# Local attention in one transformer layer pair: one more head pair as a batch of four query blocks, and a shift of one transpose step

## The chip, the cores and the metric

The kernel runs on one core of a Trainium2 chip. The metric is device microseconds per execution, measured over several runs. A core has TensorE (PE in the profile), VectorE (DVE), ScalarE (ACT), GpSimd (POOL) and SyncE (SP, which here issues most DMAs). PE works on matrices of up to 128 rows and writes to PSUM, which has eight banks of 128 x 512 float32.

## The reference

Two layers, each of: a SwiGLU feed-forward, layer norm, a token mixer, layer norm, a second feed-forward, layer norm. The sequence is 512 tokens of width 1024. The token mixer has three branches of 8 heads of width 64: NSA (compressed, selected and windowed attention), SWA (local attention in windows of 128 with a sink), and FOX (attention with a forget gate). Two of them matter here. Local attention, cut to its core:

```python
kk, vv = with_prev(k), with_prev(v)              # block before, and own block
logits = einsum('bnqghd,bnkgd->bghnqk', q, kk) * scale
logits = where(mask, logits + bias, -inf)
p = softmax(concatenate([logits, sink], -1))[..., :-1]
o = einsum('bghnqk,bnkgd->bnqghd', p, vv)
```

and the compression of NSA's keys and values, whose result the NSA branch needs before its first scores:

```python
flat = blocks.reshape(B, G, nc, CMP_BLOCK * dh)  # 32 positions x 64
return gelu(flat @ w1) @ w2                      # 2048 x 256, 256 x 64
```

## The kernel before

The kernel is one long list of instructions written with a tile framework. `tc.manual_schedule(engines={PE, POOL})` (L89) keeps PE's and POOL's instructions in the order in which the program lists them; a planner orders those of ACT, DVE and SP, with earlier listed instructions ranked higher. Tiles come from tags: a tag has a fixed number of slots, which are used again and again. The tag `p` has 13 slots (`PB`, L753) and serves the probability tiles of all branches, the compression weights (`cw1`, `cw2`), their inputs (`z`) and the GELU's tiles (`gl`, `glt`).

In `mix`, the attention of all branches and the projections that feed it run together. Projections are cut into chunks of 128 columns, each of eight parts of three products (`pj`, 0.7 us a part), and stand in one queue, `fill`. `pump(n)` runs n parts from its head. Some entries of the queue are free: they run with the part behind them and aren't counted.

Attention runs in batches of units. A unit of local attention is `Swa(m, qb)`: head pair m (0 to 3), query block qb (0 to 3). Its `s` makes scores (`sS`, into PSUM tag `sc` with three banks) and the softmax on DVE, ACT and POOL; its `tr` transposes the probabilities on PE (`ptS`, into PSUM tag `tp` with two banks) and evacuates them; its `pv` multiplies by the values (`po`). `step(cur, prev, n)` (L1417) interleaves the scores of batch `cur`, the transposes of the batch before, `prev`, and n pumped parts. It divides them into slots: one score product per slot, then about half of the slot's pumped parts, then transposes in pairs, then the other half. At the end `values()` (L1440) multiplies the batch before by its values. If `prev` is local attention and there are more than twice as many slots as pairs of transposes, the step is `early`: transposes go in the middle slots, and `values()` after the second last slot. `PUMPS` (L1472) says how many parts each step pumps. The batches before are: head pairs 0 and 1 as two batches of two query blocks each, head pairs 2 and 3 as one batch of four each, then thirteen steps of Fox and NSA units.

The compression is fed between. `conv` (L915) takes `cw1` in 16 pieces k, each of two DMAs (L930) and a product into PSUM tile `hid` (L937). `feed` (L962) issues one piece's loads if fewer than four pieces wait in `narrow`. Free entries that call it stand in the queue before each part of the second and third chunk of local queries behind the first two (CQB2, CQB3) and of the first Fox query and key chunks (L1366 to L1369), and nowhere else. `values()` runs what waits in `narrow`, after the value products (L1445). The entry that closes the compression, `end` (L968), is put into the queue five parts before the end of the first NSA query chunk (L1373). It feeds and multiplies what is left, and then transposes the result of the GELU (`glT`, L951). The GELU's five instructions (L941 to L945) are listed behind the product of the last piece, k = 15.

The selected-key chunks of NSA (CKV2, CKV4) come before that query chunk. Each is evacuated into two `hl` tiles (L829 on ACT, L830 on DVE) and copied into its key tile by eight DMAs on SP (L836).

Of the kernel before, what the change touches and what calls it, by code (L numbers as in the profile page):

```python
# [66 lines left out]
def body(tc, a, out, depth=DEPTH):  # L67
# [15 lines left out]
    def ps(tag=None, name="ps", shape=(P, 512)):  # L83
        if tag is None:
            tag = PS_ALL[ring[0] % 8]
            ring[0] += 1
        return psp.tile(list(shape), F32, name=name, tag=tag, bufs=PS_TAGS[tag])
# [663 lines left out]
    def mix(l, wts, pend, done_ffn, xap, xa, nxt):  # L751
# [585 lines left out]
        def pump(n=1):  # L1337
            while n > 0 and fill:
                n -= fill.popleft()() is not FREE
# [58 lines left out]
        def need(u):  # L1398
            if u.br == 1:
                return u.m in m.qb and hasattr(m, "kb")  # L1400
            if u.br == 2:
                return u.m in m.qc and u.m in m.kc and u.m in m.vc and u.m in m.nck
            return u.m in m.qa and hasattr(m, "c2")

        batches = []
        for i in range(4):
            u = [Swa(i, qb) for qb in range(4)]
            batches += [u[0:2], u[2:4]] if i < 2 else [u]
        for i in range(4):
            batches.append([c(i, qb) for qb in (0, 1) for c in (Fox, Nsa)])  # L1410
            batches += [[Fox(i, qb), Nsa(i, qb)] for qb in (2, 3)]
# [1 line left out]
        def chain(gens):  # L1413
            for g in gens:
                yield from g

        def step(cur, prev, n):  # L1417


            for u in cur:  # L1420
                while not need(u):
                    pump(1)
                    n -= 1
            it, iu = chain(u.tr() for u in prev), chain(u.s() for u in cur)
            nt, ns = sum(u.ngrp for u in prev), sum(u.nseg for u in cur)
            pair = 2
            nt = (nt + pair - 1) // pair
            both = 2 if ns == 2 else 1
            ns //= both
            slots = max(nt, ns, 1)  # L1430
            done = 0

            def upto(x):
                nonlocal done
                x = int(round(x))
                if x > done:
                    pump(x - done)
                    done = x

            def values():  # L1440
                if prev:
                    po = ps("po", "po", (P, 4, P))
                    for j, u in enumerate(prev):
                        u.pv(po[:, j])
                    while narrow:  # L1445
                        narrow.popleft()()
                    for j, u in enumerate(prev):
                        nc.scalar.activation(o_t[u.br][u.m][:, u.qb * P:(u.qb + 1) * P], po[:, j], AF.Copy)

            early = prev and isinstance(prev[0], Swa) and slots > 2 * nt  # L1450
            last = min(2, max(n, 0))
            n -= last
            for j in range(slots):
                if j * ns // slots != (j + 1) * ns // slots or slots == ns:
                    for _ in range(both):
                        next(iu, None)
                upto(n * (2 * j + 1) / (2 * slots))
                if (abs(j - slots // 2) < 2 if early else j * nt // slots != (j + 1) * nt // slots or slots == nt):
                    for _ in range(pair):
                        next(it, None)  # L1460
                upto(n * (j + 1) / slots)
                if early and j == slots - 2:
                    values()
            for _ in iu:
                pass
            for _ in it:
                pass
            pump(last)
            if not early:
                values()  # L1470

        PUMPS = [13, 13, 9, 9, 18, 18] + [11, 10, 11] * 4 + [8]  # L1472
        for cur, prev, n in zip(batches + [[]], [[]] + batches, PUMPS):
            step(cur, prev, n)
        while fill:
# [34 lines left out]
        early = deque(["sc", "tp", "sc", "tp", "sc"])  # L1510
# [251 lines left out]
    for l in range(depth):  # L1762
        fin = l == depth - 1
        wts, pend, done, xap, xa = ffn(l, a["ffn1_w1"][l], a["ffn1_w2"][l], 0, xap, xa, wts, pend, done, False,
                                       lambda: mix_first(l), None if l else late)
        wts, pend, done, xap, xa = mix(l, wts, pend, done, xap, xa, lambda: ffn_first(a["ffn2_w1"][l]))
        wts, pend, done, xap, xa = ffn(l, a["ffn2_w1"][l], a["ffn2_w2"][l], 2, xap, xa, wts, pend, done, fin,
                                       lambda: None if fin else ffn_first(a["ffn1_w1"][l + 1]))
# [30 lines left out]
```

## Time and profile before

| | |
|---|---|
| median of three runs | 2409.51 us (2409.47 to 2410.24) |
| the profiled execution | 2409.0 us |
| its span, first to last instruction | 2407.3 us |
| PE busy | 2397.4 us, 100% of the span |
| PE weight loads busy | 2161.8 us, 90% |
| DVE busy | 1960.1 us, 81% |
| ACT busy | 1237.6 us, 51% |
| POOL busy | 298.7 us, 12% |
| granted clock of PE, mean | 0.999 |
| DMA | 319.84 MB, mean 133 GB/s |

Products on PE are pipelined and their ends are modelled, so that a busy PE isn't PE at its peak; the start of one row to the start of the next says more than a row's duration. In a timeline row the columns are start, duration, engine, source line, operation, output and inputs, shape, number of merged instructions, and in brackets the idle time before it and what ended it. A row of the waits is: who waited, on whom, total us, times, longest. SPq is SP's queue of DMA issues; its rows give the issue, not the transfer. PE rows of 32-bit products count each product twice, as it is run in two passes. Layer 0's mixer begins its local attention at about 394 us, layer 1's some 1195 us later.

### The profile page before, as it was taken

Reading aid. Unit: us, or ns where it says so; the run is one execution under the profiler, and the core shown is the slowest. Engines: PE = TensorE matmul, PEld = TensorE weight load, DVE = VectorE, ACT = ScalarE, POOL = GpSimd, SP = SyncE. Lnnn points to the kernel's source line nnn. Section 1 sums busy time; section 2 is a strip of 40 time slices with the busy share of each in tenths; the row PEclk is TensorE's granted clock in tenths of the full one; section 3 lists DMA queues with packets and bytes.
Section 4 is the critical chain, followed back from the end, with each engine's and each line's share of the span. In section 5 each row is a group of like instructions: output and inputs, shape, how many; then the busy total and the mean of one; then the engine's idle time right before and its main releaser. Section 6 shows DMA issues by size and latency. Waiting matters only on the chain.

```text
span 2407.3 us, 42309 instructions
## 1 busy us (share of the span) xinstructions
PE 2397.4 (100%) x16129; PEld 2161.8 (90%) x16129; DVE 1960.1 (81%) x3834; ACT 1237.6 (51%) x2257; POOL 298.7 (12%) x514
## 2 busy tenths in 40 slices
PE   9999999999999999999999999999999999999998
PEld 9999888888889899998899998878888898999987
DVE  7997975787688689888799979667777886898796
ACT  4444644576644435445444446445766444444463
POOL 2000322133300000001100002121332000000021
PEclk9999999999999999999999999999999999999999
DMA  6332975632134433337733339645321344233394
GB/s 204 103 109 90 256 212 162 176 93 81 45 105 132 136 102 114 106 115 211 200 106 108 112 111 243 195 132 150 101 74 55 104 133 147 89 115 106 97 238 147
DMA packets 402155, 319.84 MB, mean 133 GB/s; under 512 B 18536, under 2 KB 348664, under 8 KB 401952
## 3 DMA queue, kind: packets, MB, share of 16 engines
q1 hardware_dynamic: 381424, 267.07, 37.3%
q0 software_dynamic: 20528, 50.07, 9.0%
q8 instruction: 127, 2.08, 0.4%
q14 instruction: 76, 0.62, 0.1%
HBM read 289.77 MB, written 17.88 MB: 128 GB/s over the span
## 4 chain that ended last, share of the span: by engine, by line
PE 99%; DMA 0%; DVE 0%; issue 0%; POOL 0%; SPq 0%; POOLq 0%; ACT 0%; DVEq 0%
PE pg L382 22%; PE acc L487 13%; PE pu L382 11%; PE acc L195 9%; PE pj L181 6%; PE pj L183 6%; PE pj L182 6%; PE pv L382 6%; PE brp L181 2%; PE brp L182 2%; PE brp L183 2%; PE sN L1187 2%; PE ptN L1229 1%; PE po L1248 1%; PE po L1135 1%; PE sF L1104 1%
## 5 line engine op out<-in xcount | busy, mean ns | idle before, releaser
L161 DVE TENSOR_TENSOR lo<-raw,hi 128x1024 fp32r<-128x1024 f32 x272 | 332.8, 1227 | 104.7 <-ACT hi L160 104.3
L160 ACT ACTIVATE hi<-raw 128x1024 fp32r<-128x1024 f32 x272 | 285.7, 1055 | 209.2 <-PE pg L382 53.5
L382 PE MATMUL pg<-xh,lo 128*128 128x256 f32 x1104 | 312.5, 283 | 0.0
L382 PE MATMUL pg<-xl,hi 128*128 128x256 f32 x1104 | 312.4, 283 | 0.0
L382 PE MATMUL pg<-xh,hi 128*128 128x256 f32 x1104 | 312.3, 283 | 0.0
L181 PE MATMUL pj<-xh,hi 128*128 128x512 f32 (+1 forms) x720 | 265.8, 369 | 0.5 <-ACT hi L1625 0.5
L364 ACT ACTIVATE hi<-ws 128x1024 fp32r<-128x1024 f32 x184 | 191.8, 1055 | 127.4 <-DVE ws L360 59.7
L183 PE MATMUL pj<-xh,lo 128*128 128x512 f32 (+1 forms) x720 | 254.6, 354 | 0.0
L182 PE MATMUL pj<-xl,hi 128*128 128x512 f32 (+1 forms) x720 | 254.5, 353 | 0.0
L365 DVE TENSOR_TENSOR lo<-ws,hi 128x1024 fp32r<-128x1024 f32 x184 | 223.3, 1222 | 34.5 <-ACT hi L364 34.2
L382 PEld LDWEIGHTS pg<-xl,hi 128*128 128x128 f32 x1104 | 211.9, 192 | 0.8
L382 PEld LDWEIGHTS pg<-xh,hi 128*128 128x128 f32 x1104 | 211.9, 192 | 0.8
L382 PEld LDWEIGHTS pg<-xh,lo 128*128 128x128 f32 x1104 | 211.9, 192 | 0.0
L382 PE MATMUL pu<-th,hi 128*128 128x256 f32 x608 | 172.1, 283 | 0.0
L382 PE MATMUL pu<-th,lo 128*128 128x256 f32 x608 | 172.1, 283 | 0.0
L382 PE MATMUL pu<-tl,hi 128*128 128x256 f32 x608 | 172.1, 283 | 0.0
L462 POOL DMA_DIRECT2D bt<-in_ffn_w_dram x32 | 40.9, 1808 | 939.3 <-DVE lo L161 938.8
L183 PEld LDWEIGHTS pj<-xh,lo 128*128 128x128 f32 x720 | 136.1, 189 | 19.8 <-DVE lo L1626 0.2
L367 ACT ACTIVATE dh<-raw 128x512 fp32r<-128x512 f32 x92 | 58.1, 632 | 184.2 <-PE pv L382 124.5
L181 PEld LDWEIGHTS pj<-xh,hi 128*128 128x128 f32 x720 | 136.4, 189 | 15.5 <-issue 2.7
L182 PEld LDWEIGHTS pj<-xl,hi 128*128 128x128 f32 x720 | 136.7, 190 | 11.5 <-DVE xl L1711 0.2
L487 PE MATMUL acc<-hi,xh 128*128 128x512 f32 x384 | 118.3, 389 | 0.0
(409 smaller groups left out, 6655.5 us busy)
## 6 DMA issues: line engine op xcount, KB each, us to landing
raw<-in_ffn_w_dram SPq DMA_DIRECT2D x232, 512.0 KB, 4.0
raw<-in_w_in_dram SPq DMA_DIRECT2D x56, 512.0 KB, 4.1
raw<-in_w_gate_dram SPq DMA_DIRECT2D x48, 512.0 KB, 3.9
b<-in_ffn_w_dram SPq DMA_DIRECT2D x32, 512.0 KB, 8.0
bt<-in_ffn_w_dram POOLq DMA_DIRECT2D x32, 512.0 KB, 8.4
x_sp<-xa POOLq DMA_DIRECT2D x24, 512.0 KB, 5.8
ks<-hl SPq DMA_DIRECT2D x96, 128.0 KB, 2.4
bt<-in_ffn_w_dram SPq DMA_DIRECT2D x16, 512.0 KB, 10.1
```

The costliest lines, as they stand in the source:

```text
L160: lnq.hi = nc.scalar.activation(hi[:, c], raw[:, c], AF.Copy).ins
L161: lnq.lo = nc.vector.tensor_tensor(lo[:, c], raw[:, c], hi[:, c].bitcast(F32), op=OP.subtract).ins
L181: nc.tensor.matmul(o, hi[:, k], vh, start=first, stop=False)
L182: nc.tensor.matmul(o, hi[:, k], vl, start=False, stop=False)
L183: nc.tensor.matmul(o, lo[:, k], vh, start=False, stop=last)
L195: nc.tensor.matmul(o, x(k)[:, t], y[:, c], start=first and i == 0, stop=last and i == 2, skip_group_check=True)
L364: pa = nc.scalar.activation(hi, x, AF.Copy)
L365: pv = tt(lo, x, hi.bitcast(F32), op=OP.subtract)
L367: nc.scalar.activation(ud[0], ru[:, h2], AF.Copy)
L382: nc.tensor.matmul(o, wx, vx, start=first and k == 0 and i == 0, stop=k == 3 and i == 2, skip_group_check=True)
L487: nc.tensor.matmul(o[t], u[:, k, s], v[:, c], start=first and j == 0 and i == 0, stop=False, skip_group_check=True)
L1187: nc.tensor.matmul(o[:, 0:nb].rearrange("p k b j -> p (k b j)"), q, kx[:, 2 * b0:2 * (b0 + nb)].rearrange("p a b -> p (a b)"), start=i == ...
```

## The change

Head pair 1 becomes one batch of four query blocks, as head pairs 2 and 3 are; only head pair 0 stays in two batches. The pump counts follow: one step of 18 parts takes the place of two of 9. In an early step the transposes were tried in the slots around the middle, j = 3, 4, 5 of 8 (1, 2, 3 of 4); they now go into the middle slot and the one two before it, j = 2 and 4 of 8 (0 and 2 of 4).

```diff
-            batches += [u[0:2], u[2:4]] if i < 2 else [u]
+            batches += [u[0:2], u[2:4]] if i < 1 else [u]
...
-                if (abs(j - slots // 2) < 2 if early else j * nt // slots != (j + 1) * nt // slots or slots == nt):
+                if (j in (slots // 2 - 2, slots // 2) if early else j * nt // slots != (j + 1) * nt // slots or slots == nt):
...
-        PUMPS = [13, 13, 9, 9, 18, 18] + [11, 10, 11] * 4 + [8]
+        PUMPS = [13, 13, 18, 18, 18] + [11, 10, 11] * 4 + [8]
```

With these counts the last batch of local attention is transposed in a step of eight slots (the first Fox and NSA units), and the first pair's transposes come one score product earlier than before; the second pair stays where it was.

## The prediction

> **What bounds the kernel now.** First the page: span and chain.
>
> ```profile
> span 2407.3 us, 42309 instructions
> ...
> PE 99%; DMA 0%; DVE 0%; issue 0%; POOL 0%; SPq 0%; POOLq 0%; ACT 0%; DVEq 0%
> ```
>
> The chain that ended last is TensorE (PE) for 99% of the span. So a step is worth what it does to PE's own stream, and every pause of PE is paid in full. Next the waits of PE:
>
> ```profile
> PE ptS L1065 <- DVE p L1071: 0.5, 2, 0.3
> ...
> PE ptS L1065 <- DVE p L801: 0.3, 2, 0.2
> ```
>
> Next to none are left in 2407 us, and of these 0.8 us belong to the transposes of local attention (ptS), which the change moves. PE's timeline shows their place in layer 0 (layer 1 repeats it):
>
> ```profile
> 475.57 0.60 PE L1065 MATMUL ptS<-ident,p 128*128 128x128 f32 x4
> 475.93 0.48 PE L1104 MATMUL sF<-ks,qs 128*128 128x256 f32 x2
> 476.56 0.41 PE L1065 MATMUL ptS<-ident,p 128*128 128x128 f32 x2 [0.15 <-DVE p L801]
> 477.22 0.41 PE L1065 MATMUL ptS<-ident,p 128*128 128x128 f32 x2 [0.25 <-DVE p L1071]
> ```
>
> Two pairs of transposes stand around one score product, and the second pair waits until the first leaves its two PSUM banks. While it waits, projection products stand ready behind it and are not pulled forward: PE works in the order in which the program lists it.
>
> **The gains.** The changed rule puts the two pairs at j = 2 and j = 4, with two score products and pumped projection work between them. Before, the two sF take 0.63 us from start to the next start (475.93 to 476.56). Two such score records elsewhere take 0.34 (436.81 to 437.15, next fence): 0.29 lost. Two transposes then take 0.66 (476.56 to 477.22) where four take 0.36 (475.57 to 475.93), so 0.18: 0.48 lost. The move is worth 0.77 us per layer. What hides the evacuation afterwards is that work between the pairs: more than the 1.3 us from 475.93 to 477.22 in which both banks emptied here.
>
> The joined batch saves one step with its values product and one run of the compression products (hid) beside it:
>
> ```profile
> 433.96 0.39 PE L183 MATMUL pj<-xh,lo 128*128 128x512 f32 x1
> 434.28 0.88 PE L1078 MATMUL po<-p,v 128*64 128x128 f32 x12
> 434.99 1.90 PE L937 MATMUL hid<-cw,z 128*64 128x256 f32 x16
> 436.81 0.51 PE L1029 MATMUL sS<-ks,qs 128*128 128x256 f32 x2
> 437.15 0.40 PE L181 MATMUL pj<-xh,hi 128*128 128x512 f32 x1
> 437.39 0.39 PE L182 MATMUL pj<-xl,hi 128*128 128x512 f32 x1
> ```
>
> Products pj follow each other at 0.23 us; into po it is 0.32, and the first two sS behind hid take 0.34 where two take 0.24 (454.31 to 454.54, next fence). Entry and exit cost about 0.2 us, saved once per layer. Splitting Swa's scores into four places costs nothing: four sS take 0.47 (457.29 to 457.76). The numbers of instructions on ACT, DVE and POOL do not change. Gains: 2 x (0.77 + 0.2) = 1.9 us.
>
> **The cost: the last four compression loads.** Feeding is tied to the batches: a `feed` entry loads one k of cw1 if fewer than four wait (L964), and only `values` (L1445) runs those that wait. The feeds end with the last part of the Fox key chunk. Before, `values` runs four times around them: k 0-3, 4-7, 8-11, 12-15, the last inside the step of the third head pair. Working the pump counts through by hand for the changed list (13, 13, 18, 18, 18), the joined batch removes one `values`: k 0-3, 4-7, 8-11, the last at the end of the third pair's step, and no feed entry is left then. So k 12-15 fall to the closing entry `end` (L968, put into the queue at L1373), which loads and multiplies them on the spot, runs the GELU on the result, and at once transposes it (glT). PE then has, in its list: hid 12-15, glT, with nothing between. Before, this was:
>
> ```profile
> 447.82 1.90 PE L937 MATMUL hid<-cw,z 128*64 128x256 f32 x16
> ...
> 454.31 0.40 PE L1029 MATMUL sS<-ks,qs 128*128 128x256 f32 x2
> 454.54 0.40 PE L181 MATMUL pj<-xh,hi 128*128 128x512 f32 x1
> ...
> 457.29 0.64 PE L1033 MATMUL sS<-ks,qs 128*128 128x256 f32 x4
> 457.76 0.40 PE L181 MATMUL pj<-xh,hi 128*128 128x512 f32 x1
> ...
> 460.30 0.38 PE L951 MATMUL glT<-ident,gl 128*128 128x128 f32 x2
> ```
>
> The cover that goes is 10.6 us, from the end of hid (449.72) to glT. Two waits take its place.
>
> GELU, a chain of five:
>
> ```profile
> 449.79 0.39 ACT L941 ACTIVATE gl<-hid 128x256 f32<-128x256 f32 x1 [1.31 <-PE hid L937]
> 450.21 0.29 DVE L942 TENSOR_SCALAR gl<-gl 128x256 f32<-128x256 f32 x1 [1.05 <-ACT gl L941]
> ...
> 451.12 0.42 DVE L943 TENSOR_TENSOR gl<-gl,hid 128x256 f32<-128x256 f32 x1
> ...
> 452.53 0.40 ACT L944 ACTIVATE gl<-gl 128x256 f32<-128x256 f32 x1
> ...
> 453.80 0.41 DVE L945 SCALAR_TENSOR_TENSOR gl<-gl,hid 128x256 f32<-128x256 f32 x1
> ```
>
> The five sum to 1.91 us; with the hop of 0.03 seen between the first two, and 0.07 from PE into ACT (449.72 to 449.79), 2.1 us at least; with other work between them, as here, 4.4 (449.79 to 454.21). I take 2.1: with PE standing, ACT and DVE run out of other work.
>
> The loads. T is the start of the fourth pair's first score, 454.31. PE reaches `end` at T+6.0 (460.30), the instructions between being the same. When do the loads get issued?
>
> ```profile
> 355.04 2.54 SPq L787 DMA_DIRECT2D tab<-bvec  x3
> ...
> 387.53 1.09 SPq L923 DMA_DIRECT2D cw<-in_cmp_k_w_dram  x2
> ```
>
> The bias tables, with slots of their own, are loaded as soon as their pool is there; the first load into the shared tag p (cw2) is held 32 us longer, although its 13 slots are nearly empty. I read this as slots of a tag being given in program order, so that a load waits in the planning for the tile ahead of it. The first cw1 loads agree: they sit behind a later weight load, beside the first DVE work on the tile ahead of them:
>
> ```profile
> 406.80 0.57 SPq L930 DMA_DIRECT2D cw<-in_cmp_k_w_dram  x1
> ```
> ```profile
> 406.97 0.41 DVE L1004 CUSTOM_DVE_ANT_0 p<-sS,tab 128x256 f32<-128x256 f32 x1
> ```
>
> For k 12 that tile is Swa(3,1)'s, first written by L1004 at 458.06, T+3.75. By then SP has other work of higher rank:
>
> ```profile
> 458.06 0.42 DVE L1004 CUSTOM_DVE_ANT_0 p<-sS,tab 128x256 f32<-128x256 f32 x1 [0.46 <-PE sS L1033]
> 458.23 0.58 ACT L829 ACTIVATE hl<-pj 128x512 fp32r<-128x512 f32 x1
> ...
> 460.96 0.68 DVE L830 TENSOR_TENSOR hl<-pj,hl 128x512 fp32r<-128x512 f32 x1
> ```
> ```profile
> 453.44 11.47 SPq L836 DMA_DIRECT2D ks<-hl  x16
> 464.95 1.37 SPq L167 DMA_DIRECT2D raw<-in_w_in_dram  x2
> ```
>
> The eight ks copies of the second selected-key chunk need hl of L829 (ready T+4.5) and L830 (T+7.3), and are traced before `end`. At 0.72 us each (11.47/16) the first four occupy SP to T+7.4 and the last four to T+10.3. Eight cw1 issues take 3.8 us, 435.63 to 439.47, and land 3.6 us after issue:
>
> ```profile
> 435.63 0.52 SPq L930 DMA_DIRECT2D cw<-in_cmp_k_w_dram  x1
> ...
> 439.07 0.40 SPq L930 DMA_DIRECT2D cw<-in_cmp_v_w_dram  x1
> ```
> ```profile
> DMA to landing us min/median/max: 2.2/3.6/4.6
> ```
>
> So the last load is issued at T+10.3+3.4 = T+13.7, lands at T+17.3, and its hid ((436.81 - 434.99)/4 = 0.46) ends at T+17.8. With 2.1 us of GELU, glT starts at T+19.9; without waits it would start at T+6.0+1.8 = T+7.8. The wait is 12.1 us per layer, 24.2 in both.
>
> Its lower end: all eight loads ahead of the eight copies. SP is free of the first chunk's copies at about T+1.0. That chunk ended 12 pj (2.7 us) before T, at 451.6, and its copies began 1.9 us later and took 8 x 0.72 = 5.8; in the new order one pair's transposes (0.4), the values of four blocks (28 records at 0.71/12: 1.7) and hid (1.8) come between as well, so it ends 6.6 to 6.7 before T. The last load is issued at T+4.4 and lands at T+8.0; hid 15 would start at T+7.4 anyway, so 0.6 us plus 2.1 of GELU: 2.7 per layer. The upper end: the two weight loads that waited behind the copies (1.37 us) get in first as well, a landing of 4.6 and a GELU of 4.4: 12.1 + 1.4 + 1.0 + 2.3 = 16.8. I take 12.1, as ranks and ready times put the copies first.
>
> The sum, against the profiled execution's own 2409.0 us (median of the runs 2409.5): 2409.0 - 1.9 + 24.2 = 2431.3.
>
> **A rule of the Trainium skill.** PE in its first 7 us:
>
> ```profile
> 1.11 3.66 PE L1607 MATMUL warm<-xl 128*128 128x128 f32 x16 [1.11 <-DVE xl L1602]
> ...
> 5.82 1.06 PE L1607 MATMUL warm<-xl 128*128 128x128 f32 x8
> ```
>
> Sixteen records from rest take 0.23 us each, eight of the same a little later 0.13: starting from rest costs 16 x 0.10 = 1.6 us. The trace has no later pause near this one's, so whether the predicted wait of 8 us before hid 12 brings that pace back can't be read from it. In the Trainium skill, "TensorE: Matmul & The Clock Gate", Part 1 (the HAM clock gate), the array falls to half rate after an idle window of about 3.4 us and returns after as long a busy one. That speaks against this change, and the warm-up rows agree with its second half; by its figures a return costs half of 3.4, some 1.7 us, an estimate, and the sum would be 2434.7.
>
> **Rivals.** (1) The pace falls in the pause too: 1.6 us more per layer by the warm-up rows, 2434.5. For it: the start. Against it: the profile of before shows no such pause.
>
> (2) The loads get ahead of the copies: 2 x 2.7 to 2 x 5.0 (with the slow GELU) - 1.9, so +3.5 to +8.1: 2412.5 to 2417.1. For it: SP has a gap from T+1.0 to T+4.5 and the loads read nothing but the slots. Against it: cw2 was held for 32 us.
>
> (3) Not slower: the planner lets PE pass `end`, running the nine pj and the score that follow. They are 2.5 us of work, and cover the GELU if the loads are early. Then only the gains remain: 2409.0 - 1.9 = 2407.1. It decides as soon as the wait falls below 1 us per layer. Against it: PE waited at 476.56 with such work behind it.
>
> **Chances.** Late loads as summed 0.40; with the slow pace 0.35; early loads 0.18; no wait 0.04; something unseen 0.03. A measurement of this kernel tells 0.2% (4.8 us) from no change; no wait (-1.9) and a third of the early loads (up to 2413.8) lie within it. Slower 0.89, same 0.10, faster 0.01. The range: down to 2415, the middle of the early case, up to 2440, which takes in the slow pace and all but the last of the wait's upper end (2409.0 - 1.9 + 2 x 16.8 = 2440.7). Outside remain half of early loads (0.09), no wait (0.04) and the far tail (0.06).
>
> **What would show it.** In the changed profile: sixteen hid records directly before glT in each layer, PE's waits headed by hid <- DMA cw and glt <- DVE gl (L945), some 9 us and 2 us each; eight cw1 issues on SP behind the ks copies; ptS with no wait at the last batch. Warm pj at 0.23 us behind the pause would refute rival 1, a hid run with no wait the late loads. A fourth hid run ahead of `end` would make the whole cost wrong, and a change in PE's stretches elsewhere would mean that I missed a place.

## The result, and the profile after

The changed kernel takes 2433.5 us (median; 2432.47 to 2434.46), the kernel before 2409.49 us beside it (2409.16 to 2410.24). The ratio is 1.0099, with a 95% interval of 1.0088 to 1.0111: 24.0 us slower. The profiled execution took 2433.97 us with a span of 2432.0 us. Its mean granted clock is 0.994, where before it was 0.999; that small number turns out to matter.

The page's chain, and PE's waits (who waited, on whom, total us, times, longest):

```profile
PE 98%; DMA 1%; SPq 1%; DVE 1%; issue 0%; ACT 0%; POOL 0%; DVEq 0%; POOLq 0%; ACTq 0%
```
```profile
PE hid L937 <- DMA cw<-in_cmp_k_w_dram: 11.3, 4, 4.9
PE glT L951 <- DVE gl L945: 4.5, 2, 2.2
```

The chain, 99% PE before, now passes through a DMA, SP's queue and DVE. The two waits are those that the prediction named, and the waits of ptS are gone. The first wait looks too small, 11.3 us in two layers where some 18 were forecast. But the last twelve hid records (465.99, below) span 3.92 us, where sixteen took 1.90 before: part of the waiting stands in their row as busy time (and a smaller part is the slow clock of which more below). So the loss is better read from landmarks in PE's order, which both kernels share. The landmarks, in PE's timeline of after, are the first score of the second head pair, of the fourth (T in the prediction), glT, and the next two values products of local attention:

```profile
416.59 0.50 PE L1029 MATMUL sS<-ks,qs 128*128 128x256 f32 x2
...
452.55 0.51 PE L1029 MATMUL sS<-ks,qs 128*128 128x256 f32 x2
...
459.95 1.17 PE L937 MATMUL hid<-cw,z 128*64 128x256 f32 x4 [1.18 <-DMA cw<-in_cmp_k_w_dram]
465.99 3.92 PE L937 MATMUL hid<-cw,z 128*64 128x256 f32 x12 [4.87 <-DMA cw<-in_cmp_k_w_dram]
472.14 0.69 PE L951 MATMUL glT<-ident,gl 128*128 128x128 f32 x2 [2.23 <-DVE gl L945]
...
482.66 1.75 PE L1078 MATMUL po<-p,v 128*64 128x128 f32 x28
...
493.05 1.75 PE L1078 MATMUL po<-p,v 128*64 128x128 f32 x28
...
1623.16 0.50 PE L1029 MATMUL sS<-ks,qs 128*128 128x256 f32 x2
...
1659.13 0.51 PE L1029 MATMUL sS<-ks,qs 128*128 128x256 f32 x2
...
1671.59 3.84 PE L937 MATMUL hid<-cw,z 128*64 128x256 f32 x12 [3.88 <-DMA cw<-in_cmp_k_w_dram]
1677.66 0.69 PE L951 MATMUL glT<-ident,gl 128*128 128x128 f32 x2 [2.23 <-DVE gl L945]
1689.48 1.75 PE L1078 MATMUL po<-p,v 128*64 128x128 f32 x28
1699.88 1.75 PE L1078 MATMUL po<-p,v 128*64 128x128 f32 x28
```

The same places of the kernel before, as far as they are not in the prediction (454.31 and 460.30 are there):

```profile
416.08 0.51 PE L1029 MATMUL sS<-ks,qs 128*128 128x256 f32 x2
...
469.39 1.75 PE L1078 MATMUL po<-p,v 128*64 128x128 f32 x28
480.56 1.75 PE L1078 MATMUL po<-p,v 128*64 128x128 f32 x28
...
1610.94 0.51 PE L1029 MATMUL sS<-ks,qs 128*128 128x256 f32 x2
...
1649.02 0.40 PE L1029 MATMUL sS<-ks,qs 128*128 128x256 f32 x2
1655.01 0.38 PE L951 MATMUL glT<-ident,gl 128*128 128x128 f32 x2
1664.11 1.75 PE L1078 MATMUL po<-p,v 128*64 128x128 f32 x28
1675.27 1.75 PE L1078 MATMUL po<-p,v 128*64 128x128 f32 x28
```

Subtracting gives, in us (the fourth hid run, 1.82 us, moves from the first stretch into the second; the last column takes it out of both):

| stretch | layer | before | after | change without the moved hid |
|---|---|---|---|---|
| second to fourth pair's first score | 0 | 38.23 | 35.96 | -0.45 |
| | 1 | 38.08 | 35.97 | -0.29 |
| fourth pair's first score to glT | 0 | 5.99 | 19.59 | +11.78 |
| | 1 | 5.99 | 18.53 | +10.72 |
| glT to the next values product | 0 | 9.09 | 10.52 | +1.43 |
| | 1 | 9.10 | 11.82 | +2.72 |
| from there to the next one | 0 | 11.17 | 10.39 | -0.78 |
| | 1 | 11.16 | 10.40 | -0.76 |

The column sums to +24.4. The profiled executions differ by 25.0, their spans by 24.7; nearly 0.5 of the rest is the very first projection product of the kernel, which starts at 7.81 us here and at 7.33 before, in code that the change doesn't touch.

The second stretch is the pause ahead of glT. SP's queue in it:

```profile
456.05 0.41 SPq L930 DMA_DIRECT2D cw<-in_cmp_k_w_dram  x1
456.51 0.43 SPq L930 DMA_DIRECT2D cw<-in_cmp_v_w_dram  x1
458.25 5.30 SPq L836 DMA_DIRECT2D ks<-hl  x8
463.65 0.56 SPq L930 DMA_DIRECT2D cw<-in_cmp_k_w_dram  x1
...
466.16 0.43 SPq L930 DMA_DIRECT2D cw<-in_cmp_v_w_dram  x1
```

The loads of k 12 slip in ahead of the eight ks copies, those of k 13 to 15 come right behind them; the last is issued at T+13.6 (in layer 1, in the same order, at T+13.0). Between 456.94 and 458.25 SP issues nothing, and k 13 doesn't use the gap. The GELU's first and last instruction:

```profile
469.95 0.38 ACT L941 ACTIVATE gl<-hid 128x256 f32<-128x256 f32 x1 [8.80 <-PE hid L937]
```
```profile
471.67 0.42 DVE L945 SCALAR_TENSOR_TENSOR gl<-gl,hid 128x256 f32<-128x256 f32 x1 [0.48 <-ACT gl L944]
```

2.14 us from the start of the one to the end of the other.

The third stretch has no wait at all, and yet is longer. PE's timeline behind glT, and the table of short windows (length, busy us of PE, weight loads, DVE, ACT and POOL, then the granted clock, the DMA share and GB/s):

```profile
473.49 0.63 PE L181 MATMUL pj<-xh,hi 128*128 128x512 f32 x1
473.91 0.63 PE L182 MATMUL pj<-xl,hi 128*128 128x512 f32 x1
...
475.41 0.39 PE L183 MATMUL pj<-xh,lo 128*128 128x512 f32 x1
475.63 0.39 PE L181 MATMUL pj<-xh,hi 128*128 128x512 f32 x1
```
```profile
472.00:474.00 2.00, 1.86 (x8) 1.76 (x9) 0.78 (x4) 0.00 (x0) 0.00 (x0) 0.50 0.04 8
...
476.00:478.00 2.00, 2.00 (x20) 1.79 (x19) 0.84 (x4) 0.84 (x6) 0.37 (x1) 1.00 0.00 0
...
1680.00:1682.00 2.00, 2.00 (x7) 1.52 (x6) 0.93 (x6) 0.97 (x5) 0.00 (x0) 0.50 0.00 0
```

The same product takes 0.42 us to the next start while the granted clock is 0.50, and 0.22 when it is back at 1.00. Layer 1 (last row) shows the same clock behind its glT. This is a loss that a table of waits can't show: a busy PE at half pace waits for nobody.

### The profile page after: what moved, and what is told of

It is laid out like the page before. It is cut to its first block, busy times and chain, and to the rows that moved or that the text cites. A ratio compares the mean times of both kernels' runs of the same rounds, so it can differ in the third digit from the quotient of the medians.

```text
span 2432.0 us, 42290 instructions
## 1 busy us (share of the span) xinstructions
PE 2406.5 (99%) x16129; PEld 2167.2 (89%) x16129; DVE 1962.1 (81%) x3834; ACT 1237.8 (51%) x2257; POOL 297.4 (12%) x514
## 4 chain that ended last, share of the span: by engine, by line
PE 98%; DMA 1%; SPq 1%; DVE 1%; issue 0%; ACT 0%; POOL 0%; DVEq 0%; POOLq 0%; ACTq 0%
PE pg L382 22%; PE acc L487 13%; PE pu L382 11%; PE acc L195 9%; PE pj L181 6%; PE pj L183 6%; PE pj L182 6%; PE pv L382 5%; PE brp L181 2%; PE brp L182 2%; PE brp L183 2%; PE sN L1187 2%; PE ptN L1229 1%; PE po L1248 1%; PE po L1135 1%; PE sF L1104 1%
```

## The experiments

Two theories stood at the start. **Loads and clock:** the cost is the four pieces that `end` has to fetch late, because they are given slots of the tag p late, plus PE's half clock behind the pause. **Loads alone:** the same without the clock. A third possibility was that something else in the joined batch or in the moved transposes costs time. All ratios below are against runs of the kernel before on the same chip (2409.37 us for rule_only, join_only, starved and own_space; 2409.22 for the other three).

**1. The two halves of the change, each alone.** rule_only is the kernel before with the new rule for the transposes; join_only is the changed kernel with the old rule.

```diff
-  if (abs(j - slots // 2) < 2 if early else ...):
+  if (j in (slots // 2 - 2, slots // 2) if early else ...):
```

> The batches and pump counts of before, with the new rule for the transposes' slots alone. Theory (the cost is the last four compression pieces, the rule only gains): the two waits of the last batch's transposes go, 0.77 us per layer, so 2409.5 - 1.5 = 2408.0, and the compression runs four times as before. Rival (the moved transposes are what costs): 2420 or more.

> The joined batch and its pump counts, with the old rule for the transposes' slots. Theory: the whole cost and the small gain of one values step less stay, the 1.5 us of the rule are not gained: 2433.5 + 1.5 = 2435.0, with PE's waits on cw1 and on the GELU as in the changed kernel, and the two transposes' waits of before back. Rival (the rule and the join cost only together): near 2409.

Measured: rule_only 2407.72 us, ratio 0.9993 (0.9985 to 1.0002); join_only 2434.76 us, ratio 1.0105 (1.0090 to 1.0121). PE's waits in rule_only and in join_only:

```profile
PE warm L1607 <- DVE xl L1602: 1.1, 1, 1.1
```
```profile
PE ptS L1065 <- DVE p L1071: 0.5, 2, 0.3
```

With the new rule nothing is left but the wait of the kernel's start; with the old rule the transposes wait as before. The whole cost belongs to the joined batch, and the rule is worth some 1.7 us by the medians (its ratio alone doesn't exclude zero; the two stretches of 0.78 and 0.76 us in the profile above are the better evidence, and in the same stretch rule_only's profile has 10.39 us in both layers, join_only's 11.17).

**2. The cost without the joined batch.** starved is the kernel before, whose feed entries stop at k = 12, so that `end` has to fetch 12 to 15.

```diff
-            def feed():
-                if c.n < 16 and len(narrow) < 4:
+            def feed(most=12):
+                if c.n < most and len(narrow) < 4:
...
-                    feed()
+                    feed(16)
```

> The kernel before, batches and rule untouched, but feed stops at the twelfth piece, so that k 12 to 15 fall to the closing entry. Theory: the cost comes without the joined batch: hid and glT waits of the changed kernel, its slow clock, so 2409.5 + 26.6 = 2436, between 2433 and 2438. Rival (the joined batch of four itself costs, by taking the slots of tag p from the softmax): 2409 to 2412, as only the GELU would be uncovered.

Measured: 2437.65 us, ratio 1.0116 (1.0102 to 1.0129). PE's waits:

```profile
PE hid L937 <- DMA cw<-in_cmp_v_w_dram: 10.1, 2, 5.5
PE glT L951 <- DVE gl L945: 4.5, 2, 2.2
```

The same two waits, with four batches of two query blocks still in place. So the cost doesn't need the joined batch: it comes when the feeding runs dry. That it is 28.3 us here, 2.9 more than in join_only, was not followed up.

**3. The loads given a place of their own.** own_space is the changed kernel, with pieces 12 to 15 loaded into four output tiles of the NSA branch, which are unused until that branch's first values, instead of into slots of p.

```diff
             def load(k):
-                r = at.tile([P, 2, 256], F32, name="cw1", tag="p", bufs=PB)
+                if k < 12:
+                    r = at.tile([P, 2, 256], F32, name="cw1", tag="p", bufs=PB)
+                else:
+                    r = o_t[0][k - 12].rearrange("p (i f) -> p i f", i=2)
```

> The changed kernel, with the weights of k 12 to 15 loaded into four output tiles of the NSA branch that are unused until later, so that their loads wait for no slot of tag p. The products and the GELU stay where the change put them. Theory: the loads go out early and hid doesn't wait; the GELU's wait of 2.2 us per layer stays, too short to bring the slow clock: 2409.5 - 2.3 + 4.5 = 2411.7 and a mean clock of 0.999. Rival (the products at that place cost by themselves, or the loads are slow for another reason than their slots): 2425 or more.

Measured: 2414.58 us, ratio 1.0022 (1.0013 to 1.0031), 2.9 us above what was expected. SP's queue, PE's waits, and PE's timeline in layer 0:

```profile
361.99 0.34 SPq L933 DMA_DIRECT2D o<-in_cmp_k_w_dram  x1
```
```profile
PE glT L954 <- DVE gl L948: 4.5, 2, 2.3
```
```profile
458.80 1.95 PE L940 MATMUL hid<-o,z 128*64 128x256 f32 x16
463.01 0.44 PE L954 MATMUL glT<-ident,gl 128*128 128x128 f32 x2 [2.27 <-DVE gl L948]
...
464.45 0.63 PE L181 MATMUL pj<-xh,hi 128*128 128x512 f32 x1
464.88 0.63 PE L182 MATMUL pj<-xl,hi 128*128 128x512 f32 x1
```

The program lists these loads where it did, yet they are issued 94 us earlier (361.99 against 456.05). So it was the slots of p that held them. Whether by their order, as the prediction read it, or because they were still occupied, this run doesn't tell. No wait for a load is left; the GELU's wait stays, 4.5 us in two layers, as it must while nothing stands between hid and glT. What was missed is in the last two rows: behind a pause of only 2.27 us, layer 0 has products 0.43 us apart. Layer 1 has the same pause, and full clock (the first row is of layer 0, the second of layer 1, columns as above):

```profile
464.00:466.00 2.00, 2.00 (x7) 1.64 (x6) 1.60 (x8) 0.39 (x2) 0.00 (x0) 0.61 0.87 219
...
1662.00:1664.00 2.00, 2.00 (x12) 1.65 (x12) 1.10 (x7) 0.91 (x5) 0.00 (x0) 1.00 0.94 254
```

From glT to the next values product layer 0 takes 10.74 us, 1.65 above the 9.09 of before, and layer 1 9.17. The GELU's 4.5 and this 1.65, less the 1.5 of the moved transposes, are 4.65 of the 5.2 us by which this kernel is slower than before. The profile is that of the fastest of ten executions (2413.97 to 2416.01 us, mean granted clock 0.999 in four and 0.998 in six), so what the half clock costs in the others isn't known.

**4. The pause kept, but PE kept busy in it.** busy_pause is the changed kernel with products that nobody uses: 20 between hid 12 and hid 13, where PE waits for loads, and 8 ahead of glT, where it waits for the GELU. They do no part of the computation.

```diff
+            def busy(n):
+                j = ps("po", "junk")
+                for _ in range(n):
+                    nc.tensor.matmul(j, xh[:, 0, 0:P], xh[:, 0], start=True, stop=True)
...
                     feed()
+                    if c.n == 14:
+                        busy(20)
                     narrow.popleft()()
+                busy(8)
                 tr()
```

> The changed kernel with 20 extra 512-column products into an unused PSUM bank between the products of k 12 and 13, and 8 more between k 15 and the transposes of the GELU: some 4.6 and 1.8 us of work that fits into the waits. Theory (the pause also halves PE's clock for some us behind it): the waits stay in length, hid being paced by its loads, the clock stays at 1.00, and the 1.4 and 2.7 us that the stretches behind glT lost in the two layers come back, with some tenths of hid and glT: 2433.5 - 4.7 = 2428.8, between 2427.5 and 2430. Rival (the slow clock lies in the waits and costs nothing): 2433.5.

Measured: 2428.84 us, ratio 1.0082 (1.0068 to 1.0096). PE's timeline in layer 0, and a window of it:

```profile
452.72 0.51 PE L1037 MATMUL sS<-ks,qs 128*128 128x256 f32 x2
...
461.06 4.83 PE L971 MATMUL junk<-xh 128*128 128x512 f32 x20
466.03 3.33 PE L937 MATMUL hid<-cw,z 128*64 128x256 f32 x12
469.29 2.11 PE L971 MATMUL junk<-xh 128*128 128x512 f32 x8
471.59 0.44 PE L951 MATMUL glT<-ident,gl 128*128 128x128 f32 x2 [0.19 <-DVE gl L945]
...
480.74 1.75 PE L1086 MATMUL po<-p,v 128*64 128x128 f32 x28
```
```profile
470.00:474.00 4.00, 3.81 (x21) 2.91 (x20) 2.61 (x11) 0.42 (x1) 0.00 (x0) 1.00 0.04 10
```

More work for PE, and the kernel is faster by 4.4 us (24.0 against 19.6 over before). The last load is issued at T+13.5 and T+12.8 in the two layers, where the changed kernel has T+13.6 and T+13.0, so the loads hardly come earlier; the clock stays at 1.00. From T to glT it takes 18.87 us here, against 19.59, and from there to the values product 9.15 against 10.52. Layer 1 gives 18.44 and 9.17 against 18.53 and 11.82. So the half clock costs 0.7 + 1.4 in layer 0 and 0.1 + 2.65 in layer 1, 4.8 us by the two profiles, of which up to 0.3 may belong to the slightly earlier loads. "Loads alone" falls.

own_busy does the same to own_space: eight such products ahead of glT.

> own_space with 8 extra products in the GELU's wait. In own_space layer 0 lost 1.65 us behind glT at a clock near 0.5 after a pause of 2.27 us, and layer 1 none after an equal one. Theory (a pause of 2.3 us can bring the slow clock, depending on where it falls): no slow stretch in either layer, 2414.6 - 1.7 = 2412.9 or a little less. Rival (the loss behind glT has another cause, such as the evacuations of glT): 2414.6.

Measured: 2413.68 us, ratio 1.0018 (1.0009 to 1.0027). A window of it in layer 0, behind glT:

```profile
463.00:467.00 4.00, 3.45 (x21) 2.98 (x22) 2.54 (x11) 0.89 (x6) 0.00 (x0) 1.00 0.87 224
```

The clock stays at 1.00, and glT to the next values product takes 9.17 us where own_space took 10.74. Of these 1.6 us only 0.75 show in the differences from before (4.46 against 5.21): DVE does other work 0.55 us later in this layer, the GELU comes behind that work, and the way from T to glT takes 10.95 us instead of 10.37. The intervals of own_space and own_busy overlap, and the profiled execution of own_busy isn't the shorter one (2414.27 us beside 2413.97; it has 2.5 us of waits elsewhere that the other lacks). One profile of each couldn't settle it either, as layer 1 of own_space kept its clock without any filling. What speaks for the theory is the mean granted clock of all executions: 0.999 or 1.000 in the ten of own_busy, 0.998 in six of the ten of own_space.

**5. The joined batch with its feeding restored.** fourth_run is the changed kernel; the step that scores the batch after a full batch of local attention also multiplies the waiting pieces behind its second slot and feeds four new ones. That gives back the fourth hid run.

```diff
+                    if j == 1 and len(prev) == 4 and isinstance(prev[0], Swa):
+                        while narrow:
+                            narrow.popleft()()
+                        for _ in range(4):
+                            feed()
```

> The changed kernel with the fourth run of the compression put back: in the second slot of a step whose batch before is a full one, the waiting pieces (k 8 to 11) are multiplied behind the transposes and k 12 to 15 are fed; the values product of that step then multiplies them, a full nine pumped parts before the closing entry. Theory: no wait on hid or glT, and all gains stay: the stretches that gained lost 2.3 us against before in the changed kernel's profile, so 2409.4 - 2.3 = 2407.1, no slower than rule_only (2407.7). Rival (four query blocks, four pieces and four probability tiles at once run short of the 13 slots and stall PE): 2410 or more, with waits of sS.

Measured: 2407.64 us, ratio 0.9994 (0.9985 to 1.0003). PE's timeline in layer 0:

```profile
439.77 1.95 PE L937 MATMUL hid<-cw,z 128*64 128x256 f32 x16
...
453.07 1.90 PE L937 MATMUL hid<-cw,z 128*64 128x256 f32 x16
```

The extra run at 439.77 lets the last one (453.07) end ahead of T, as before, and PE's only waits in the whole kernel are 1.1 and 0.7 us at its start. The cost is gone, so nothing beside the late loads, the uncovered GELU and the clock is left to explain. But the time is that of rule_only, 2407.72: the joined batch brings nothing measurable of its own (in the profiles the first stretch of the table takes 38.01 and 38.00 us here and 38.08 and 38.09 in rule_only, some 0.1 less per layer). Neither kernel can be told from before by its ratio.

## Why the prediction was right, and where it wasn't

It said slower, 2431.3 us, within 2415 to 2440; measured 2433.5. By its steps:

- **The bound.** Right: PE's pauses were paid in full.
- **The rule for the transposes, 0.77 us per layer.** Right: 0.78 and 0.76 in the table, and the waits of ptS are gone.
- **The joined batch, 0.2 us per layer.** Too large. The stretch did shrink, by 0.45 and 0.29, but with the fourth hid run restored (fourth_run) some 0.1 remains by the profiles and nothing measurable in the time. So most of it isn't a gain of joining. It may lie in the entry and exit of the hid run that left this stretch for the pause; no run tested that alone.
- **k 12 to 15 fall to `end`, with glT directly behind.** Right, shown by the profile and by starved from the other side.
- **When the loads are issued.** The last one was forecast at T+13.7 and came at T+13.6 (T+13.0 in layer 1), but not quite on the forecast way: k 12 went ahead of the copies. That the slots hold the loads is shown by own_space, that it is their order that does is not. Whether k 13 to 15 waited behind the copies for rank or for slots is not settled: SP stood idle for 1.3 us without issuing them, so at first it wasn't rank that held them; afterwards it was busy with copies.
- **The wait, 12.1 us per layer.** With the clock kept up (busy_pause) the same stretch less its 7.81 us without waits gives 11.06 and 10.63, 21.7 in both where the step had 24.2. The GELU's 2.1 was right (2.14). Too long was the way from the last issue to the end of hid 15: 4.1 us were forecast (a landing of 3.6 and a product of 0.46). In busy_pause that issue is at 466.20, and hid ends at about 469.3: 3.1 (3.3 in layer 1).
- **Rival 1, the slow pace.** This is the step that failed: the sum took the pace as unharmed, and the pace fell. It costs 4.8 us, not the 3.2 that rival 1 had from the warm-up rows. Those rows were poor support anyway: their products are slow, but over them (1 to 5 us) the profile gives the granted clock as 1.00, so they don't show the half clock. The granted clock could not be forecast from rows of before, whose mixers have no such pause. In the Trainium skill, "TensorE: Matmul & The Clock Gate", Part 1 (the HAM clock gate), a half rate follows an idle window of about 3.4 us. The granted clock of 0.50 behind the pauses of 4.87 and 3.88 us agrees with it, and the forecast would have done well to follow it.

That 2431.3 came so near is partly luck, as the errors cancel: the likeliest case had 2.5 too much in the wait and 0.4 too little in the gains, and left out 4.8 for the clock. With gains of 1.5 (transposes) and 0.7 (the table's first stretch), 21.7 of waits and 4.8 of clock the profiles give +24.3, beside 24.0 measured. By its number the result lies between the likeliest case and rival 1 (2434.5); by mechanism it was rival 1.

## What to carry to other kernels

When work rides on another loop (here the feeding on the batches), count how often it runs after the loop is cut, and follow what is left over to the place that closes it: four pieces left over, of 0.46 us of products each, cost 24 us in two layers, because their loads then came late, the GELU lost its cover and the clock fell. A load whose tile comes out of a shared tag can be held by the slots of that tag while its queue is idle; a place of its own brought it 94 us forward. And price a pause of PE as its length plus half of the busy time that falls under the half clock behind it, which stands in the granted clock and in no table of waits.

## What the runs showed of the hardware that was not expected

- A pause of 2.27 us was enough for the half clock in one layer of own_space (0.61 in the window from 464), while an equal pause in the other layer left it at 1.00. That is less than the 3.4 us of the Trainium skill, "TensorE: Matmul & The Clock Gate", Part 1 (the HAM clock gate). What decides between the two layers stays open; no run here varied where the pause falls.
- The price of a pause isn't proportional to its length. After the long pauses of the changed kernel the stretch behind glT lost 1.43 us in layer 0 and 2.72 in layer 1, although layer 0 paused longer.
- The half clock lasted for whole steps. Added up from windows of 0.5 us, it stood for 3.42 us in own_space (layer 0), for 10.23 or 10.24 us in layer 0 of the changed kernel and in both layers of join_only and starved, and for 13.65 us in layer 1 of the changed kernel: one, three and four times 3.41. In the changed kernel it ended some 3.0 us behind the start of glT in layer 0 and some 5.8 us in layer 1. Half of these, 1.5 and 2.9 us, is near the 1.43 and 2.72 lost there; so in this profile it was the end of the slow stretch, and not the length of the pause, that set the price.
